# Seven products per weight pair: which accumulator banks share a tile, and how far TensorE's written order reaches

## The chip, the cores and the metric

One core of one Trainium2 chip runs the whole program. The metric is device time in microseconds (us), the median over several runs of the kernel; beside it stands one profiled execution, from which all rows below are read.

## The reference, cut to what matters

The reference is one layer of a streaming encoder over 1024 frames of width 1024: a normalisation, one wide input projection, three token mixers (HGRN2, mLSTM, Mamba-2), three sigmoid branch gates, an output projection, and a gated MLP with a causal convolution. Two products of it matter here:

```
gates = sigmoid(h @ w_in[:, gate columns])                 # 24 blocks of 128 columns
u = causal_dwconv(rmsnorm(x) @ w_up, ffn_conv_w, b)        # 44 blocks of 128 columns
x = x + (silu(u_g) * u_v) @ w_down
```

Both multiply a fixed activation matrix (1024 x 1024) by blocks of 128 weight columns, in float32.

## The kernel before

**Precision.** Each float32 operand is split into a high and a low part (`split`, L98 to L100: a ScalarE cast at L99 for the high part, a VectorE subtraction at L100 for the low one), and each product is three TensorE products: high times high, high times low, low times high.

**Pairs.** Most blocks of the gates (16 of 24) and of the up-projection (38 of 44) are computed two at a time by `pair_gemm`, as a 2 x 2 block product in seven products in place of eight (the Strassen-Winograd scheme). There are 8 pairs in the gate stage (`gate_pairs`) and 19 in the up stage (`up_pairs`). A product (`product`, L166 to L172) is 12 matmuls of 128x512, all recorded at L171, so a pair is 84 of them. In `seven` they are, in order, here called P1 to P7:

- P1 into bank x; `keep` (L188, ScalarE) copies x to the SBUF tile u0
- P2 into bank y; VectorE (L183) adds y and u0 into the first half of the output block `oa`
- P3 on top of x; `keep` copies x to u1
- P4 into bank z; VectorE adds z to u1
- P5 on top of x; `keep` copies x to u2; VectorE adds z and u2 into the second half of `ob`
- P6 into bank v; VectorE adds v and u1 into the second half of `oa`
- P7 on top of x; ScalarE copies x (L192) into the first half of `ob`

P1 and P2 use the weight tiles `wa`, P3 and P4 the tiles `s12`, P5 and P6 the tiles `s34`, P7 the tiles `qb`. `operands` (L142 to L164) makes these: two loads by SyncE's queue, the splits, and four VectorE sums and differences of weights (L160). `wa` and `s12` take turns in two buffers of one pool (`ws`), so the `wa` of one pair lies where that of the pair before lay, and can be cast when that pair's P2 has ended. After a pair, the gate stage applies a sigmoid (L832), the up stage the convolution of both blocks (ScalarE L601, VectorE L605), a SiLU (L958) and a product (L959), and each stores its result.

**Tiles in PSUM.** There are two pools: `pg` with 2 buffers of two banks (name `ps_g`) and `pm` with 4 buffers of one bank (name `ps_m`). A pair takes one `ps_g` tile, whose halves are x and y, and two `ps_m` tiles, z and v.

**The order of the work.** The framework's scheduler sets the order of the instructions on each engine ahead of the run, by a model of their times, and puts in the waits that the tiles' reads and writes ask for. Inside `manual_schedule` the instructions of the engines named are kept in the order in which they are written. Here the block holds one pair's seven products, for TensorE alone, so that the scheduler may still place matmuls from outside the block (another pair's among them) between them. `weight` and `operands` run at a raised priority.

The instruction before and after the pair stages on TensorE is L136 (`steps`), the plain product of one block, into `ps_g` tiles. Line L1001 is the VectorE addition that empties such a tile in `down`.

Of the kernel before, what the change touches and what calls it, by code (L numbers as in the profile page):

```python
# [9 lines left out]
F32 = mybir.dt.float32  # L10
# [8 lines left out]
P = 128  # L19
# [3 lines left out]
HALF = 512  # L23
# [24 lines left out]
class Trunk:  # L48
# [125 lines left out]
    def pair_gemm(self, pool, srcs, outs):  # L174

        nc = self.nc
        wa, s12, s34, qb = self.operands(pool, srcs)
        ps = self.pg.tile([P, T], F32, name="ps_g")
        x, y = ps[:, 0:HALF], ps[:, HALF:]
        z, v = (self.pm.tile([P, HALF], F32, name="ps_m") for _ in range(2))  # L180
        oa, ob = outs
        tmp = lambda: pool.tile([P, HALF], F32, name="u", bufs=4)
        add = lambda out, p, q: nc.vector.tensor_tensor(out=out, in0=p, in1=q, op=ALU.add)  # L183
        u = []

        def keep():
            u.append(tmp())
            nc.scalar.copy(out=u[-1], in_=x)  # L188

        with self.tc.manual_schedule(engines={mybir.EngineType.PE}):  # L190
            self.seven(wa, s12, s34, qb, (x, y, z, v), u, keep, add, oa, ob)
        nc.scalar.copy(out=ob[:, 0:HALF], in_=x)  # L192

    def seven(self, wa, s12, s34, qb, banks, u, keep, add, oa, ob):
        b11, b21, b22, t1, t2, t3, t4 = self.bs
# [645 lines left out]
            self.keep(self.gate_d[i], g)  # L841

    def gate_pairs(self, pool, some):
        for i in some:
            cs = [pool.tile([P, T], F32, name="c", bufs=3) for _ in range(2)]
            self.pair_gemm(pool, [self.ins["w_gate"][i + j] for j in range(2)], cs)
            for j in range(2):
                self.gate_end(i + j, cs[j])
# [120 lines left out]
            self.act(f, us)  # L969

    def up_pairs(self, pool, fs):
        for f in fs:
            ns = (2 * f, 2 * f + 1)
            cs = [pool.tile([P, T], F32, name="c", bufs=3) for _ in ns]
            self.pair_gemm(pool, [self.ins["w_up"][n] for n in ns], cs)
            us = []
            for n, c in zip(ns, cs):
                us.append(self.gp.tile([P, T], F32, name="gate", bufs=3))
                self.up_conv(us[-1], c, n)
            self.act(f, us)  # L980
# [264 lines left out]
```

## Time and profile before

| what | value |
|---|---|
| runs | 2537.37 us median of 3 (2536.49 to 2537.75) |
| the profiled execution | 2535.01 us, its span 2533.2 us |
| granted TensorE clock, mean over the span | 0.995 |
| TensorE busy | 2474.8 us of the span (98%) |
| VectorE, ScalarE busy | 1503.5 us (59%), 1003.5 us (40%) |

The gate pairs run from about 1255 to 1422 us of the span, the up pairs from about 1883 to 2277 us. A matmul row lasts longer (389 ns) than the distance to the next one, as the ends are modelled and matmuls overlap; so time on TensorE is read from start to start.

### The profile page before, as it was taken

How to read it: one execution, taken by the hardware profiler on the slowest of the kernel's cores; microseconds unless marked ns; L12 is line 12 of the kernel's file. 1: busy time of each engine (PE TensorE's matmuls, PEld its weight loads, DVE VectorE, ACT ScalarE, POOL GpSimd, SP SyncE). 2: the span in 40 equal slices, each digit the busy share in tenths (PEclk: the TensorE clock that was granted, in tenths of full speed). 3: DMA queues.
4: the chain of work that ended last, by engine and by line, in shares of the span. 5: the costliest groups of instructions: out<-in, count | busy, mean ns of one | idle time of the engine just before them, and what ended most of it. 6: DMA issues, size and time to landing. Idle time of an engine off the chain costs nothing.

```text
span 2533.2 us, 31151 instructions
## 1 busy us (share of the span) xinstructions
PE 2474.8 (98%) x12980; PEld 2111.6 (83%) x12980; DVE 1503.5 (59%) x1888; ACT 1003.5 (40%) x1233; POOL 62.2 (2%) x99
## 2 busy tenths in 40 slices
PE   8999999999999999999999999999999999999998
PEld 6898989898898898899877888888777777778886
DVE  6676767774344366766844324444687777775445
ACT  5444445553334255446433312212344444441112
POOL 2000000000000000000000000000000000000000
PEclk8999999999999999999999999999999999999999
DMA  5111111111111122122323444444222222244321
GB/s 215 34 41 44 42 42 34 53 59 58 67 67 60 49 92 80 61 69 92 150 100 105 162 134 156 156 135 150 100 76 82 75 75 77 82 136 147 108 75 67
DMA packets 64141, 228.63 MB, mean 90 GB/s; under 512 B 7400, under 2 KB 8040, under 8 KB 63232
## 3 DMA queue, kind: packets, MB, share of 16 engines
q1 hardware_dynamic: 52352, 181.54, 21.6%
q0 software_dynamic: 11648, 45.09, 4.5%
q8 instruction: 102, 1.67, 0.3%
q14 instruction: 39, 0.32, 0.0%
HBM read 177.23 MB, written 49.38 MB: 89 GB/s over the span
## 4 chain that ended last, share of the span: by engine, by line
PE 94%; DVE 2%; ACT 2%; issue 1%; DMA 1%; POOL 0%; DVEq 0%; ACTq 0%
PE ps_g L136 48%; PE ps_g L171 14%; PE ps_g L270 10%; PE ps_m L171 6%; PE ps_m L136 5%; PE ps_m L464 3%; PE ps_m L797 1%; ACT w_hi L99 1%; PE ps_m L270 1%; PE ps_m L473 1%; PE ps_m L708 1%; PE ps_m L679 1%; PE ps_m L483 1%; PE ps_m L436 0%; PE ps_m L659 0%
## 5 line engine op out<-in xcount | busy, mean ns | idle before, releaser
L136 PE MATMUL ps_g<-h,w_hi 128*128 128x512 f32 x2080 | 585.0, 397 | 5.9 <-DVE h L100 3.9
L99 ACT CAST w_hi<-w_raw 128x1024 fp32r<-128x1024 f32 x209 | 218.6, 1046 | 720.4 <-PE ps_g L136 540.6
L136 PEld LDWEIGHTS ps_g<-h,w_hi 128*128 128x128 f32 x2080 | 387.7, 188 | 86.0 <-DVE h L100 4.7
L100 DVE TENSOR_TENSOR w_lo<-w_raw,w_hi 128x1024 fp32r<-128x1024 f32 x209 | 255.1, 1221 | 169.7 <-ACT w_hi L99 168.4
L136 PE MATMUL ps_g<-h,w_lo 128*128 128x512 f32 x1040 | 331.9, 395 | 0.0
L270 PE MATMUL ps_g<-w_hi,h 128*128 128x256 f32 x1408 | 261.0, 284 | 0.0
L136 PE MATMUL ps_g<-p_hi,w_hi 128*128 128x512 f32 x768 | 239.9, 390 | 5.0 <-ACT w_hi L99 2.1
L136 PE MATMUL ps_g<-p_lo,w_hi 128*128 128x512 f32 x768 | 239.2, 389 | 0.8 <-DVE p_lo L100 0.8
L136 PE MATMUL ps_g<-p_hi,w_lo 128*128 128x512 f32 x768 | 239.3, 389 | 0.0
L136 PEld LDWEIGHTS ps_g<-h,w_lo 128*128 128x128 f32 x1040 | 195.4, 188 | 40.2
L270 PEld LDWEIGHTS ps_g<-w_hi,h 128*128 128x128 f32 x1408 | 221.2, 192 | 0.6
L270 PE MATMUL ps_g<-w_lo,h 128*128 128x256 f32 x704 | 200.1, 284 | 0.0
L136 PEld LDWEIGHTS ps_g<-p_hi,w_hi 128*128 128x128 f32 x768 | 143.8, 188 | 36.9 <-ACT w_hi L99 3.4
L136 PEld LDWEIGHTS ps_g<-p_lo,w_hi 128*128 128x128 f32 x768 | 144.1, 188 | 31.3 <-DVE p_lo L100 1.1
L136 PEld LDWEIGHTS ps_g<-p_hi,w_lo 128*128 128x128 f32 x768 | 144.1, 188 | 30.1 <-DVE w_lo L100 0.3
L270 PEld LDWEIGHTS ps_g<-w_lo,h 128*128 128x128 f32 x704 | 134.9, 192 | 0.5
L188 ACT COPY u<-ps_g 128x512 f32<-128x512 f32 x81 | 45.8, 589 | 188.6 <-PE ps_g L171 186.0
L183 DVE TENSOR_TENSOR c<-ps_m,u 128x512 f32<-128x512 f32 x54 | 37.4, 692 | 129.5 <-ACT u L188 92.9
L1001 DVE TENSOR_TENSOR x<-ps_g,x 128x1024 f32<-128x1024 f32 x40 | 49.0, 1225 | 89.3 <-PE ps_g L136 88.9
L605 DVE SCALAR_TENSOR_TENSOR gate<-c,c_vec,gate 128x1023 f32<-128x1023 f32 x76 | 95.8, 1279 | 2.0 <-ACT gate L601 1.9
L100 DVE TENSOR_TENSOR p_lo<-w_raw,p_hi 128x1024 fp32r<-128x1024 f32 x48 | 58.3, 1224 | 43.5 <-ACT p_hi L99 42.8
L99 ACT CAST p_hi<-w_raw 128x1024 fp32r<-128x1024 f32 x48 | 50.4, 1050 | 84.3 <-DMA w_raw<-act_dram 30.4
(311 smaller groups left out, 4068.8 us busy)
## 6 DMA issues: line engine op xcount, KB each, us to landing
w_raw<-w_up SPq DMA_DIRECT2D x44, 512.0 KB, 3.3
w_raw<-w_hg SPq DMA_DIRECT2D x24, 512.0 KB, 3.3
w_raw<-w_v SPq DMA_DIRECT2D x24, 512.0 KB, 3.4
ta<-rows SPq DMA_DIRECT2D x24, 512.0 KB, 4.4
w_raw<-w_gate SPq DMA_DIRECT2D x24, 512.0 KB, 3.5
w_raw<-w_br SPq DMA_DIRECT2D x24, 512.0 KB, 3.8
w_raw<-y_dram SPq DMA_DIRECT2D x24, 512.0 KB, 4.4
gate<-gate_dram SPq DMA_DIRECT2D x24, 512.0 KB, 4.4
```

What stands on the lines that cost most here:

```text
L99: self.nc.scalar.copy(out=hi, in_=src)
L100: (eng or self.nc.vector).tensor_tensor(out=lo, in0=src, in1=hi.bitcast(F32), op=ALU.subtract)
L136: self.nc.tensor.matmul(out=out, lhsT=w[:, ks], rhs=rhs(part, kt, ts), start=kt == 0 and w is hi and part == 0, stop=kt == kts - 1 and w i ...
L171: self.nc.tensor.matmul(out=out, lhsT=w[x][:, ks], rhs=b[y][k], start=start and k == i == 0, stop=stop and k == 3 and i == 2, skip_group_c ...
L183: add = lambda out, p, q: nc.vector.tensor_tensor(out=out, in0=p, in1=q, op=ALU.add)
L188: nc.scalar.copy(out=u[-1], in_=x)
L270: self.nc.tensor.matmul(out=out, lhsT=self.h[hf][part][:, 4 * i + k, o:o + P], rhs=w[:, ks], start=start and k == 0 and w is hi and part = ...
L464: nc.tensor.matmul(out=pa[0:m, c], lhsT=z[:, c * P:c * P + m], rhs=part(1)[:, c], start=True, stop=True)
L473: nc.tensor.matmul(out=pa[:, j], lhsT=c3(k)[:, c + j], rhs=qs[:, c + j], start=True, stop=True)
L483: nc.tensor.matmul(out=po[:, j], lhsT=A[:, c], rhs=v[:, c, vs], start=True, stop=c == 0)
L605: end = nc.vector.scalar_tensor_tensor(out=out[:, a:ts.stop], in0=ps[:, a - d:ts.stop - d], scalar=w(d), in1=out[:, a:ts.stop], op0=ALU.mu ...
L1001: nc.vector.tensor_tensor(out=x2[j], in0=ps, in1=x2[j], op=ALU.add)
```

## The change

In `pair_gemm` the halves of the `ps_g` tile become y and v, and the two `ps_m` tiles become x and z. The number of tiles and banks that a pair takes from each pool stays. The `manual_schedule` block moves from around one call of `seven` to a generator, `in_order`, which wraps the loop over all pairs of a stage: TensorE's instructions of all 8 (or 19) pairs are kept in the order in which they are written, P1 to P7 of one pair, then P1 to P7 of the next. The block now also encloses the loads, splits, convolutions and stores of the loop's body, on other engines than the one that it names.

```diff
         ps = self.pg.tile([P, T], F32, name="ps_g")
-        x, y = ps[:, 0:HALF], ps[:, HALF:]
-        z, v = (self.pm.tile([P, HALF], F32, name="ps_m") for _ in range(2))
+        y, v = ps[:, 0:HALF], ps[:, HALF:]
+        x, z = (self.pm.tile([P, HALF], F32, name="ps_m") for _ in range(2))
...
+        self.seven(wa, s12, s34, qb, (x, y, z, v), u, keep, add, oa, ob)
+        nc.scalar.copy(out=ob[:, 0:HALF], in_=x)
+
+    def in_order(self, jobs):
+
         with self.tc.manual_schedule(engines={mybir.EngineType.PE}):
-            self.seven(wa, s12, s34, qb, (x, y, z, v), u, keep, add, oa, ob)
-        nc.scalar.copy(out=ob[:, 0:HALF], in_=x)
+            yield from jobs
...
     def gate_pairs(self, pool, some):
-        for i in some:
+        for i in self.in_order(some):
...
     def up_pairs(self, pool, fs):
-        for f in fs:
+        for f in self.in_order(fs):
```

## Rows read from the trace of the kernel before

**Rows 1.** The page: its head, and TensorE's line of part 1.
```profile
span 2533.2 us, 31151 instructions
...
PE 2474.8 (98%) x12980; PEld 2111.6 (83%) x12980; DVE 1503.5 (59%) x1888; ACT 1003.5 (40%) x1233; POOL 62.2 (2%) x99
```
**Rows 2.** Waits of TensorE in the gate pairs: total us, times, longest.
```profile
PE ps_g L171 <- DVE c L183: 5.5, 7, 0.8
PE ps_g L171 <- ACT w_hi L99: 0.9, 1, 0.9
PE ps_g L171 <- ACT u L188: 0.7, 1, 0.7
```
**Rows 3.** The same view of the up pairs.
```profile
PE ps_g L171 <- ACT w_hi L99: 16.5, 17, 1.9
PE ps_g L136 <- ACT w_hi L99: 2.1, 1, 2.1
```
**Rows 4.** Timeline, TensorE, up pairs: start, duration, operation, [idle before, releaser].
```profile
1910.78 0.50 PE L171 MATMUL ps_g<-p_hi,w_hi 128*128 128x512 f32 x1 [0.91 <-ACT w_hi L99]
...
1965.54 2.88 PE L171 MATMUL ps_g<-t,w_b 128*128 128x512 f32 x12
1968.26 0.39 PE L171 MATMUL ps_g<-p_hi,w_hi 128*128 128x512 f32 x1
...
1970.75 0.39 PE L171 MATMUL ps_g<-p_hi,w_lo 128*128 128x512 f32 x1
1972.05 0.50 PE L171 MATMUL ps_g<-p_hi,w_hi 128*128 128x512 f32 x1 [0.91 <-ACT w_hi L99]
...
1972.68 0.73 PE L171 MATMUL ps_g<-t,w_hi 128*128 128x512 f32 x2
...
2217.10 0.50 PE L171 MATMUL ps_g<-p_hi,w_hi 128*128 128x512 f32 x1 [0.91 <-ACT w_hi L99]
```
**Rows 5.** Timeline, ScalarE, the same up pair.
```profile
1968.23 0.62 ACT L99 CAST w_b<-w_raw 128x512 fp32r<-128x512 f32 x1 [0.52 <-PE ps_g L171]
1968.76 0.58 ACT L192 COPY c<-ps_g 128x512 f32<-128x512 f32 x1
1969.37 1.25 ACT L601 ACTIVATE gate<-c,c_vec 128x1024 f32<-128x1024 f32 x1
1970.95 1.04 ACT L99 CAST w_hi<-w_raw 128x1024 fp32r<-128x1024 f32 x1 [0.33 <-PE ps_g L171]
1971.90 1.05 ACT L958 ACTIVATE gate<-gate 128x1024 f32<-128x1024 f32 x1
1975.73 0.59 ACT L188 COPY u<-ps_g 128x512 f32<-128x512 f32 x1 [2.77 <-PE ps_g L171]
```
**Rows 6.** Timeline, VectorE, the same up pair.
```profile
1969.55 2.47 DVE L605 SCALAR_TENSOR_TENSOR gate<-c,c_vec,gate 128x1022 f32<-128x1022 f32 x2
1971.94 0.69 DVE L183 TENSOR_TENSOR c<-ps_g,u 128x512 f32<-128x512 f32 x1
```
**Rows 7.** Timeline, TensorE, the first up pair.
```profile
1886.65 0.50 PE L171 MATMUL ps_g<-p_hi,w_hi 128*128 128x512 f32 x1 [0.68 <-ACT u L188]
...
1890.54 0.74 PE L171 MATMUL ps_g<-t,w_hi 128*128 128x512 f32 x2 [0.85 <-DVE c L183]
```
**Rows 8.** Timeline, TensorE, gate pairs: the second and the seventh pair's P3.
```profile
1282.62 0.72 PE L171 MATMUL ps_g<-t,w_hi 128*128 128x512 f32 x2 [0.78 <-DVE c L183]
...
1383.29 0.50 PE L171 MATMUL ps_g<-t,w_hi 128*128 128x512 f32 x1 [0.78 <-DVE c L183]
```
**Rows 9.** Windows of one pair: length; PE, PEld, DVE, ACT, POOL busy; clock; DMA.
```profile
1302.76:1322.89 20.13, 19.35 (x84) 15.68 (x84) 9.90 (x12) 7.93 (x11) 1.07 (x2) 1.00 0.30 105
1951.64:1972.05 20.41, 19.50 (x84) 15.62 (x85) 15.24 (x18) 9.29 (x12) 0.53 (x1) 1.00 0.21 78
```
**Rows 10.** Timeline, TensorE, where the last up pair meets the down-projection (L136).
```profile
2259.95 0.74 PE L136 MATMUL ps_g<-p_hi,w_hi 128*128 128x512 f32 x2 [2.06 <-ACT w_hi L99]
...
2281.91 0.73 PE L136 MATMUL ps_g<-p_hi,w_hi 128*128 128x512 f32 x2 [1.61 <-DVE x L1001]
```
**Rows 11.** Timeline, ScalarE, then VectorE, first gate pair: the high and low part of its `s12`.
```profile
1258.72 1.05 ACT L99 CAST w_hi<-w_raw 128x1024 fp32r<-128x1024 f32 x1 [0.19 <-DVE w_raw L160]
...
1259.80 1.23 DVE L100 TENSOR_TENSOR w_lo<-w_raw,w_hi 128x1024 fp32r<-128x1024 f32 x1 [0.39 <-ACT w_hi L99]
```

## The prediction

> **What bounds the kernel now.** I read the head of the page first: TensorE is busy 2474.8 of 2533.2 us [rows 1], so the end is set by TensorE's own work and by the holes in it, and a change that adds and removes no matmul can only move holes. Then the waits of TensorE, taken for the two stretches that the change touches [rows 2, 3]: there the reader sees three releasers only, the cast of a weight (`w_hi` L99), the addition at L183 and the copy at L188; no DMA. Then the timeline, to see where in a pair the holes lie [rows 4 to 8].
>
> A product starts 2.72 us after the one before (P7 at 1965.54, P2 at 1968.26) [rows 4], so a pair without holes takes 7 x 2.72 = 19.04 us. The up pairs come every 20.42 us, (2217.10 - 1910.78) / 15, and the gate pairs every 20.13 us, (1383.29 - 1282.62) / 5 [rows 4, 8]. So an up pair has 1.38 us of holes and a gate pair 1.09. A hole costs some 0.3 us more than the row's idle time (1.09 against 0.78), since rows overlap; I add 0.3 to each hole below.
>
> What the up pair's hole is: after P2 has ended (last start 1970.75) two matmuls of the next pair's P1 come, then P3 (1972.68) [rows 4]. Those two stand there because the program's order puts them there. Their weight can only be cast when P2 has let go of the buffer: the cast begins at 1970.95 and takes 1.04 [rows 5], and TensorE sits 0.91 us. P3 could not have gone either: in the gate pairs, where it stands directly behind P2, it waits 0.78 us for L183, the addition that reads y [rows 8]. That addition ran at 1971.94, behind two L605 [rows 6]. But P3 writes x, not y. And in the first up pair P2, which writes y, waits 0.68 us for the copy of x [rows 7]. In both cases the waiting product shares nothing with its releaser but the tile whose halves are x and y. I read that as waits kept by tile.
>
> **The change, part by part.**
>
> *x leaves y's tile.* P2 no longer shares a tile with the copy of x, nor P3 with the addition out of y. P3 still must wait for the copy u0, as must P5 for u1 and P7 for u2. Each has a whole other product in front of it: 2.72 us, against a copy of 0.59 [rows 5] that can start about when that product starts. The cover is some 2.1 us, one 1.25 us activation can run into it free, two cannot. The new partners y and v: P6 writes v while the tile's other half was read by the addition after P2, which is 3 products or 8.2 us earlier; nothing. z keeps a tile of its own. Buffers: x now takes `ps_m`, two of four per pair, so it falls to the tile of two pairs back, whose last reader (L192) is a whole pair old; nothing.
>
> *Order over all pairs.* P1 of a pair now stands behind P7 of the one before, and not in the hole after P2. No instruction is added. Its cast becomes possible when the last P2 ends, 5 products or 13.6 us ahead of its use, against a cast of 1.04 and a subtraction of about 1.2 [rows 5, 11]. The casts of `s12` and `s34` have the same distance from the P4 and P6 that free their buffers. No load is moved past another: SyncE's queue holds loads one pair ahead before and after.
>
> What goes, with 0.3 per single hole:
> - up pairs: 17 waits for the cast. 16 regular ones at 1.38 = 22.1; the 17th is the long one, 1.9 in place of 0.91 [rows 3], 2.4.
> - first up pair: 0.68 + 0.85 + 0.6 = 2.1 [rows 7].
> - after the last up pair's P2 the down-projection's matmuls take the hole and wait 2.06 for their own cast [rows 10]: 2.4.
> - gate pairs: 7 waits for L183 at 1.09 = 7.6; the first pair's two others, 0.9 + 0.7 + 0.6 = 2.2 [rows 2].
> - together 38.8.
>
> What stays or comes:
> - first gate pair: P3 would come up about 1260.5, and its `s12` is cast by 1259.8 and subtracted by 1261.0 [rows 11], while the third matmul wants it at 1260.9. 0 to 0.6; I take 0.3.
> - behind the last P7, all eight columns of the first down group now follow at once, and VectorE has the last pair's convolutions to do beside emptying them. Now that costs 1.61 + 0.3 [rows 10], with one column done ahead. It could shrink to 0 (-1.9) or cost one L605 and one L1001 more (+2.5). I take +1.5, nearer to the upper end as more columns meet the same VectorE.
> - VectorE and ScalarE have 15.24 and 9.29 us of work in an up pair [rows 9]; over 19.04 us that is 80% and 49%. Neither becomes the bound, and no matmul hangs closely on VectorE any more.
>
> Sum: 38.8 - 0.3 - 1.5 = 37.0. The profiled execution took 2535.0 us (span 2533.2), which becomes 2498; the median of the runs lies 2.4 above it, so 2537.4 - 37 = 2500.5 us.
>
> On the tile reading a rule of the Trainium skill speaks against the first part: the page "PSUM — Partial Sum Buffer" (Terms, PSUM bank) lets TensorE's write and ScalarE's read clash only in one and the same bank. x and y lay in different banks before as well, so by that rule nothing is won by giving them other tiles, and the 0.68 us that P2 waited for the copy of x must have another cause. That would be the case of the rival "the waits stay", below. The trace shows the wait, not its cause; I hold it to be the program's, not the chip's.
>
> **The rivals.**
>
> *The copies come late.* With P1 directly behind P7, the ScalarE queue between them and u0 holds the cast `w_b` 0.62, the copy L192 0.58, L601 1.25 and the SiLU 1.05 [rows 5]: 3.5 us from P7's end, and then u0 ends at 4.1, where P3 is due at 5.44. That fits. But the SiLU needs VectorE's convolutions. If it stands ahead of u0 and waits for two L605 (2.47) [rows 6], u0 ends at 0.62 + 0.58 + 1.25 + 2.47 + 1.05 + 0.59 = 6.6, with four handovers of 0.2 at 7.4: P3 is 1.9 us late in each of 19 up pairs, 36 us, and the time is 2537; with one L605 in the way less, 0.7 late, 2514. For it: the SiLU stands before the u copy in that queue today. Against: there it started without any idle time, and the queue is laid out from times that now let the copy be ready first. Slower only if u0 ends later than 7.4 us after P7.
>
> *The order does not hold across pairs* and P1 keeps its place behind P2. Then the up pairs keep their hole, the gate pairs lose theirs (9.8): 2528. For: a matmul from outside a block is placed into it today. Against: the new block holds all pairs.
>
> *The waits stay* (the slower one). If P2's wait for the copy and P3's for the addition come from something other than the tile, the strict order lays them bare in every pair, as the first up pair has them today: 2.1 us [rows 7] x 27 = 57 us, against 38.8 removed, with the 1.8 that comes: 2537.4 + 57 - 37 = 2557. It decides from 37 / 27 = 1.4 us per pair. Against: P2's operands are older than P1's, and the releaser reads only x.
>
> **How the numbers follow.** My forecast 0.81, with a range of its own from 2495 (both open ends nil or below, 2 of slack) to 2508 (0.3 us of late copies in every pair, or the tail at its upper end with it). Late copies 0.09, 2508 to 2537; order not held 0.03, 2528; waits stay 0.07, 2557. The range 2494 to 2519 leaves out the last two, most of the late copies and a few hundredths of the forecast: under 2 in 10. 0.2% (5 us) is about what a measurement of this kernel can tell from no change: faster is 0.81 + 0.03 + 0.05 of the late copies = 0.89, same 0.04, slower 0.07.
>
> **What would show it.** In the waits of TensorE over the up pairs, the rows for `w_hi` L99 and L183 are gone, and pairs follow at 19.1 us in both stages. The product P1 into `ps_m` follows P7 directly. ScalarE's u copies begin within 0.3 us of a product's end. If the SiLU row shows idle time released by VectorE and L171 waits for L188, the first rival holds; if P2 shows a hole of 0.7 released by L188, the third. The forecast is wrong if the pair's period stays above 19.6 us, or if holes of more than 5 us appear elsewhere on TensorE.

## The result and the profile after

The changed kernel takes 2498.73 us (median of 4 runs, 2498.43 to 2500.11) against 2537.36 before: a ratio of 0.9849, 95% interval 0.9832 to 0.9866. Its profiled execution took 2498.8 us, its span 2497.0. In the experiments below the same program was run again, with 2499.3 us. The medians differ by 38.6 us, the two profiled spans by 36.2: the profiled execution before was 2.4 us faster than its median, the one after 0.1 us slower.

The head of the page after; it answers to [rows 1].

```profile
span 2497.0 us, 31129 instructions
...
PE 2464.3 (99%) x12980; PEld 2116.6 (85%) x12980; DVE 1508.2 (60%) x1888; ACT 1005.8 (40%) x1233; POOL 62.2 (2%) x99
```

As many matmuls as before (12980) end 36.2 us earlier. From the starts of the first and last L171 of each stage: the gate pairs went from 166.50 to 158.46 us, the up pairs from 393.12 to 364.25, what lies between the stages stayed at 461.6, and what follows went from 257.0 to 256.6. The gate pairs begin 1.1 us later, at 1256.13; in the second run of the same program they begin at 1255.50, so two runs of one program differ by 0.6 us here.

The waits of TensorE after, first over the gate pairs, then over the up pairs and the start of the down-projection. These two rows are all that is left of [rows 2, 3].

```profile
PE ps_m L171 <- DVE w_lo L100: 1.5, 1, 1.5
```
```profile
PE ps_g L136 <- DVE x L1005: 2.2, 1, 2.2
```

TensorE's timeline after, from P7 of one up pair to P1 of the next but one; it answers to [rows 4].

```profile
1949.59 2.88 PE L171 MATMUL ps_m<-t,w_b 128*128 128x512 f32 x12
1952.31 0.39 PE L171 MATMUL ps_m<-p_hi,w_hi 128*128 128x512 f32 x1
...
1955.03 0.39 PE L171 MATMUL ps_g<-p_hi,w_hi 128*128 128x512 f32 x1
...
1957.75 0.61 PE L171 MATMUL ps_m<-t,w_hi 128*128 128x512 f32 x2
...
1971.35 0.39 PE L171 MATMUL ps_m<-p_hi,w_hi 128*128 128x512 f32 x1
```

P7, P1, P2 and P3 start 2.72 us apart without an idle note, and P1 comes again after 1971.35 - 1952.31 = 19.04 us: 7 x 2.72, a pair without a hole. The window of that pair, with the columns of [rows 9]:

```profile
1952.31:1971.35 19.04, 19.04 (x85) 15.77 (x84) 15.55 (x18) 9.39 (x12) 0.53 (x1) 1.00 0.24 83
```

ScalarE and VectorE in the same pair, against [rows 5, 6]:

```profile
1952.29 0.62 ACT L99 CAST w_b<-w_raw 128x512 fp32r<-128x512 f32 x1 [0.52 <-PE ps_m L171]
1952.81 0.58 ACT L191 COPY c<-ps_m 128x512 f32<-128x512 f32 x1
1953.43 1.25 ACT L605 ACTIVATE gate<-c,c_vec 128x1024 f32<-128x1024 f32 x1
1955.23 0.59 ACT L188 COPY u<-ps_m 128x512 f32<-128x512 f32 x1 [0.56 <-PE ps_m L171]
1955.72 1.06 ACT L962 ACTIVATE gate<-gate 128x1024 f32<-128x1024 f32 x1
```
```profile
1953.60 3.79 DVE L609 SCALAR_TENSOR_TENSOR gate<-c,c_vec,gate 128x1022 f32<-128x1022 f32 x3
1957.50 1.23 DVE L963 TENSOR_TENSOR gate<-gate 128x1024 f32<-128x1024 f32 x1
1958.64 0.68 DVE L183 TENSOR_TENSOR c<-ps_g,u 128x512 f32<-128x512 f32 x1
```

The addition out of y (L183) now runs at 1958.64, 0.9 us after P3 has begun. In the old tiles P3 would have waited for it; here it needs the copy alone, which ended at 1955.82. And the SiLU (L962) now stands behind the copy.

### The profile page after: what moved, and what is told of

It is laid out like the page before. It is cut to its first block, busy times and chain, and to the rows that moved or that the text cites. A ratio compares the mean times of both kernels' runs of the same rounds, so it can differ in the third digit from the quotient of the medians.

```text
span 2497.0 us, 31129 instructions
## 1 busy us (share of the span) xinstructions
PE 2464.3 (99%) x12980; PEld 2116.6 (85%) x12980; DVE 1508.2 (60%) x1888; ACT 1005.8 (40%) x1233; POOL 62.2 (2%) x99
## 4 chain that ended last, share of the span: by engine, by line
PE 96%; DVE 2%; issue 1%; ACT 1%; DMA 0%; SPq 0%; DVEq 0%; ACTq 0%
PE ps_g L136 48%; PE ps_m L171 15%; PE ps_g L274 10%; PE ps_g L171 6%; PE ps_m L136 5%; PE ps_m L468 3%; PE ps_m L801 1%; PE ps_m L274 1%; PE ps_m L477 1%; PE ps_m L712 1%; PE ps_m L683 1%; PE ps_m L487 1%; PE ps_m L440 1%; PE ps_m L663 0%; PE ps_m L685 0%
## 5 line engine op out<-in xcount | busy, mean ns | idle before, releaser
L136 PE MATMUL ps_g<-h,w_hi 128*128 128x512 f32 x2080 | 585.4, 398 | 5.8 <-DVE h L100 3.9
L136 PEld LDWEIGHTS ps_g<-h,w_hi 128*128 128x128 f32 x2080 | 388.2, 189 | 85.6 <-DVE h L100 4.7
L136 PE MATMUL ps_g<-h,w_lo 128*128 128x512 f32 x1040 | 332.3, 395 | 0.0
L136 PE MATMUL ps_g<-p_hi,w_hi 128*128 128x512 f32 x768 | 239.5, 390 | 2.8 <-DVE x L1005 2.2
L136 PE MATMUL ps_g<-p_lo,w_hi 128*128 128x512 f32 x768 | 239.2, 389 | 0.8 <-DVE p_lo L100 0.8
L136 PE MATMUL ps_g<-p_hi,w_lo 128*128 128x512 f32 x768 | 239.4, 389 | 0.0
L136 PEld LDWEIGHTS ps_g<-h,w_lo 128*128 128x128 f32 x1040 | 195.6, 188 | 40.3
L136 PEld LDWEIGHTS ps_g<-p_hi,w_hi 128*128 128x128 f32 x768 | 144.0, 188 | 34.0 <-DVE x L1005 2.6
L136 PEld LDWEIGHTS ps_g<-p_lo,w_hi 128*128 128x128 f32 x768 | 144.2, 188 | 31.2 <-DVE p_lo L100 1.1
L136 PEld LDWEIGHTS ps_g<-p_hi,w_lo 128*128 128x128 f32 x768 | 144.1, 188 | 30.2 <-DVE w_lo L100 0.3
L171 PE MATMUL ps_m<-t,w_hi 128*128 128x512 f32 x432 | 133.0, 389 | 0.0
L171 PEld LDWEIGHTS ps_m<-t,w_hi 128*128 128x128 f32 x432 | 81.1, 188 | 16.8
L188 ACT COPY u<-ps_m 128x512 f32<-128x512 f32 x81 | 47.6, 588 | 117.4 <-PE ps_m L171 117.4
L171 PE MATMUL ps_m<-t,w_lo 128*128 128x512 f32 x216 | 84.1, 390 | 1.5 <-DVE w_lo L100 1.5
```

The lines of the kernel that those rows point to most:

```text
L136: self.nc.tensor.matmul(out=out, lhsT=w[:, ks], rhs=rhs(part, kt, ts), start=kt == 0 and w is hi and part == 0, stop=kt == kts - 1 and w i ...
L171: self.nc.tensor.matmul(out=out, lhsT=w[x][:, ks], rhs=b[y][k], start=start and k == i == 0, stop=stop and k == 3 and i == 2, skip_group_c ...
```

## The experiments

All were run against the kernel before, which took 2537.6 to 2538.0 us beside them.

**The tiles without the order.** From the changed kernel, the block goes back around one pair:

```diff
+        with self.tc.manual_schedule(engines={mybir.EngineType.PE}):
+            self.seven(wa, s12, s34, qb, (x, y, z, v), u, keep, add, oa, ob)
...
-        for i in self.in_order(some):
+        for i in some:
```

> The new tiles, with the written order around one pair's products only, as before. Theory T (the holes came from waits that go by tile; x sharing a tile with y made P3 wait for the addition at L183, and only that hole let the next P1 in behind P2): with x in its own tile P3 can follow P2 at once, so no hole opens, the pairs run at 19.1 us in both stages, and the time is that of the changed kernel, 2499 within 5 us. Rival O (the order over all pairs is what does it): P1 of the next pair keeps its place behind P2 in the up pairs and waits there for its cast, 1.38 x 19 = 26 us stay and the gate pairs' holes go: about 2525 us.

2499.46 us (ratio 0.985, 0.9834 to 0.9867): the whole gain. The two holes that are left are those of the changed kernel (waits of TensorE, the two longest):

```profile
PE ps_g L136 <- DVE x L1006: 2.1, 1, 2.1
PE ps_m L171 <- DVE w_lo L100: 1.5, 1, 1.5
```

TensorE's order is not that of the changed kernel, though. In every pair that has a next one, the next pair's P1 and P2 stand, cut in pieces, before P5 and before P7, and in the gate pairs and about half of the up pairs behind P7 too. With x out of y's tile that costs nothing. Rival O is out.

**The order without the tiles.**

```diff
-        y, v = ps[:, 0:HALF], ps[:, HALF:]
-        x, z = (self.pm.tile([P, HALF], F32, name="ps_m") for _ in range(2))
+        x, y = ps[:, 0:HALF], ps[:, HALF:]
+        z, v = (self.pm.tile([P, HALF], F32, name="ps_m") for _ in range(2))
```

> The old tiles (x and y in one, z and v in tiles of their own), with the order written over all pairs. Theory T: every pair shows the two holes of the first up pair of the kernel before, P2 behind the copy of x (0.68 + 0.3) and P3 behind the addition out of y (0.85 + 0.3, more where VectorE is still at the convolutions): 2.1 us or more in each of 27 pairs, 57 us above the changed kernel, 2556 us or later, slower than before. Rival B (waits go by bank, the tiles don't matter): no such holes, 2499 us.

2555.44 us, slower than before (ratio 1.0074, 1.0059 to 1.0089). TensorE's waits, and its timeline in one up pair:

```profile
PE ps_g L171 <- ACT u L188: 20.7, 27, 2.2
PE ps_g L171 <- DVE c L183: 20.1, 25, 0.9
```
```profile
2000.35 0.50 PE L171 MATMUL ps_g<-p_hi,w_hi 128*128 128x512 f32 x1 [0.68 <-ACT u L188]
...
2004.16 0.74 PE L171 MATMUL ps_g<-t,w_hi 128*128 128x512 f32 x2 [0.78 <-DVE c L183]
```

The two holes of the first up pair of before [rows 7] come back in nearly every pair: P2 waits for the copy in all 27, P3 for the addition in 25 (not in the first gate pair and the last up pair). A pair takes 21.13 us, 2.09 more than 19.04; 27 of them make 56.4, and the kernel is 56.7 us slower than the changed one.

**x with v in one tile**, order over all pairs:

```diff
-        y, v = ps[:, 0:HALF], ps[:, HALF:]
-        x, z = (self.pm.tile([P, HALF], F32, name="ps_m") for _ in range(2))
+        x, v = ps[:, 0:HALF], ps[:, HALF:]
+        y, z = (self.pm.tile([P, HALF], F32, name="ps_m") for _ in range(2))
```

> Order over all pairs; x shares its tile with v, and y and z have tiles of their own. Every bank is still a separate one. Theory T: P6, which writes v, waits for the copy u2 of x that follows P5 (0.7 + 0.3), and P7, which writes x, waits for the addition out of v that follows P6 (0.8 + 0.3): 2.1 us in each of 27 pairs, 2556 us. P2 and P3 wait for nothing. Rival B (by bank): 2499 us, no hole.

2552.36 us (ratio 1.006, 1.0045 to 1.0075). Timeline of TensorE in an up pair:

```profile
2009.92 0.50 PE L171 MATMUL ps_g<-p_hi,w_s 128*128 128x512 f32 x1 [0.68 <-ACT u L188]
...
2013.73 0.50 PE L171 MATMUL ps_g<-t,w_b 128*128 128x512 f32 x1 [0.79 <-DVE c L183]
```

The waiters are now P6 (`p_hi,w_s`) and P7 (`t,w_b`); P2 and P3 wait for nothing, but for the first gate pair's P3 (1.5 us, for a weight). The holes have moved to the products that now share a tile with a bank just read, with the same length, while each bank is separate in all three kernels. So the waits go by tile, not by bank.

**y with z in one tile**, x and v alone (the same two lines, with `y, z` from `ps` and `x, v` from `self.pm`):

> Order over all pairs; x and v have tiles of their own, y and z share one. So the bank of the fifth product has no tile of its own, unlike in the changed kernel. Theory T: P4, which writes z, must wait for the addition out of y that follows P2; one whole product (2.72 us) stands between, against some 1.8 us until that addition has ended in an up pair; nothing is left over, 2499 us within 3. Rival Z (z needs a tile of its own): P4 waits in each up pair, 0.5 us or more, 2509 us or later.

2499.0 us (ratio 0.985, 0.9836 to 0.9865), and no wait of L171 in the up pairs. The fifth product's bank needs no tile of its own. What counts is that two products that follow each other don't share one: P2 and P4 share one here, and the product between them covers the wait.

**Copies made three times and six times.** In the changed kernel:

```diff
-            nc.scalar.copy(out=u[-1], in_=x)
+            for _ in range(3):
+                nc.scalar.copy(out=u[-1], in_=x)
```

> The changed kernel, with each copy of x (u0, u1, u2) made three times into the same tile, which adds two copies of some 0.49 us to each of 81. By the forecast's cover: the copies of a product end some 0.35 + 3 x 0.49 = 1.8 us after the next product's start, the third product is due at 2.72, nothing is late: 2499 us within 4. By the rival that the copies already come late, each added copy is paid in full: 81 x 0.98 = 79 us, 2578 us; in part: anything above 2505.

2509.96 us: a miss, by 7 us beyond its bound. The gate pairs stayed 19.04 us apart. The up pairs came some 19.36 apart, but the last began 23.3 us after the one before it: there a cast for the down-projection and the SiLU both stood before the last copy, and P3 waited 2.4 us. ScalarE in one up pair:

```profile
1994.11 0.59 ACT L189 COPY u<-ps_m 128x512 f32<-128x512 f32 x1 [0.56 <-PE ps_m L171]
1994.59 1.06 ACT L963 ACTIVATE gate<-gate 128x1024 f32<-128x1024 f32 x1
1995.55 1.20 ACT L189 COPY u<-ps_m 128x512 f32<-128x512 f32 x2
```

The queue put the SiLU between the copies of u0. They end at 1996.75, and P3, due 2.72 after P2's start at 1993.91, came at 1996.81 in place of 1996.63. That is the mechanism of the first rival, at the edge of its cover: two added copies (1.20, where the expectation had 0.98) and a SiLU (1.06) just exceed what is there. Where no SiLU stands between the copies, as in the gate pairs, two added copies are free.

> The changed kernel with each copy of x made six times. By the forecast's cover: 0.35 + 6 x 0.49 = 3.3 us against 2.72, so 0.57 late, and 0.1 for the restart, in each of 81 places: 54 us, about 2553 us, with waits of L171 for L188 of some 0.4 to 0.5 us each, that weren't there before. If the cover were twice as long (5.4 us), 2499 still; if it were 1 us, 2700 or more.

2772.84 us, 220 us beyond the expectation. ScalarE, then TensorE, in one up pair; then the window of that product, and of the whole stage; then the waits of TensorE over both stages:

```profile
2107.69 2.45 ACT L189 COPY u<-ps_m 128x512 f32<-128x512 f32 x4 [3.10 <-PE ps_m L171]
2110.19 1.04 ACT L99 CAST w_hi<-w_raw 128x1024 fp32r<-128x1024 f32 x1
2111.14 1.20 ACT L189 COPY u<-ps_m 128x512 f32<-128x512 f32 x2
```
```profile
2112.38 4.61 PE L171 MATMUL ps_m<-t,w_s 128*128 128x512 f32 x12 [2.01 <-ACT u L189]
```
```profile
2112.38:2116.83 4.45, 4.45 (x12) 3.53 (x13) 0.71 (x2) 0.00 (x0) 0.00 (x0) 0.62 0.39 118
```
```profile
1949.00:2514.00 565.00, 435.93 (x1620) 335.65 (x1618) 302.77 (x323) 341.32 (x497) 10.10 (x19) 0.90 0.17 60
```
```profile
PE ps_m L171 <- ACT u L189: 175.9, 77, 3.6
```

Three things were left out of the expectation. A copy behind a copy costs 0.61 us (four take 2.45) and not 0.49, so six alone would be over 1 us late and not 0.57. A cast stands between them in the queue, so TensorE sits 2.0 us before P5; over both stages it waits 175.9 us in 77 places. And the granted clock falls: 0.62 in this product, which takes 4.45 us to the next one's start in place of 2.72, 0.90 over the up stage and 0.92 over the 242 us of the gate stage. An estimate from these: 175.9 + 77 x 0.3 for the holes and 0.10 x 565 + 0.08 x 242 for the clock make 275 us, against 273.5 measured over the changed kernel.

**The hole behind the last pair.** First, one x tile in another pool:

```diff
-                        x2.append(pool.tile([P, T], F32, name="x2", bufs=KT))
+                        x2.append(self.gp.tile([P, T], F32, name="gate", bufs=3) if j == 0 else
+                                  pool.tile([P, T], F32, name="x2", bufs=KT))
```

> The changed kernel, with the first of the eight x tiles of the down-projection in a buffer of the gate pool, which doesn't have to wait for the last pair's operands to be let go. Theory F (the hole of 2.2 us behind the last pair is the first addition L1005 waiting for that tile's load, issued at 2240.8 only when P7 has ended): the load is issued before P7, the hole shrinks to 0.5 us or less, and the time is 2 us lower, 2496.7 us. Rival V (VectorE's convolutions L609 hold the addition): the hole stays within 0.5 us of 2.2 and the time does too.

2499.81 us, and a hole of 2.28. It decides nothing between the two: SyncE's queue, here, still sends the load (into `gate`) at 2240.80, behind two of the others and when P7 had ended.

```profile
2239.83 0.80 SPq L245 DMA_DIRECT2D x<-x_dram  x2
2240.80 0.32 SPq L245 DMA_DIRECT2D gate<-x_dram  x1
```

> The changed kernel itself beside the others, for a comparison on one chip: 2498.7 us within 2.

2499.3 us. Then, in the changed kernel, two of the eight loads go into weight buffers, ahead of the others:

```diff
+            early = [self.wr.tile([P, T], F32, name="w_raw") for _ in range(2 if first == 0 else 0)]
+            for j, t in enumerate(early):
+                self.fetch(t, self.x2_d[j])
...
-                        self.fetch(x2[j], self.x2_d[j])
-                    nc.vector.tensor_tensor(out=x2[j], in0=ps, in1=x2[j], op=ALU.add)
+                        was = early[j] if j < 2 else x2[j]
+                        if j >= 2:
+                            self.fetch(was, self.x2_d[j])
+                    else:
+                        was = x2[j]
+                    nc.vector.tensor_tensor(out=x2[j], in0=ps, in1=was, op=ALU.add)
```

> The changed kernel; the first two of the eight x tiles that the down-projection adds to are loaded into two of the four weight buffers, behind the first activations' loads, so that they need not wait until the last pair's operands are let go. In the run before, the load meant to be early still went out behind P7, so it told nothing. Theory F (the hole of 2.2 us behind the last pair is L1005 waiting for that load): the two loads land before P7 ends, the hole is 0.6 us or less, 2 us are gained, 2497 us. Rival V (VectorE's convolutions hold the addition): the hole stays within 0.5 us of 2.2, 2499 us.

The first addition runs at 2241.03, with P7 started at 2237.91 in both kernels (it ran at 2244.43 in the changed one), and two small holes take the place of the one (VectorE, then TensorE):

```profile
2241.03 1.22 DVE L1012 TENSOR_TENSOR x<-ps_g,w_raw 128x1024 f32<-128x1024 f32 x1
```
```profile
2241.17 0.73 PE L136 MATMUL ps_g<-p_hi,w_hi 128*128 128x512 f32 x2 [0.38 <-DVE c L183]
...
2247.24 0.73 PE L136 MATMUL ps_g<-p_hi,w_hi 128*128 128x512 f32 x2 [0.31 <-DVE x L1012]
```

So the hole was the load (theory F). The 2 us that were expected of it did not come. Counted from the last L171, the matmuls behind the holes come 1.0 to 1.1 us earlier than in the changed kernel, and the end of the program 0.2 to 0.3 us earlier (256.27 us behind it, against 256.60 and 256.52 in the changed kernel's two profiles). The time is 2498.32 us (2496.9 to 2498.54), against 2499.3 for the changed kernel in another batch on another chip; 1 us is less than such a measurement can tell.

**The tiles without any written order.** In the changed kernel, both loops go without `in_order`, so that no `manual_schedule` is left around a pair or a stage:

> The new tiles with no written order at all, neither for a pair nor for a stage. Theory T (once x is alone in its tile nothing on TensorE waits, whatever the order among the pairs): the pairs still run at 19.1 us and the time is 2499 within 5 us. Rival O (the order inside a pair is needed): the scheduler brings products that use x next to each other, each such place costs a copy, 0.95 us, once or more in 27 pairs: 2525 us or later.

2501.64 us (ratio 0.9859, 0.9842 to 0.9875). The scheduler mixes the products of neighbouring pairs throughout (P7 in the middle of the next pair's P3 and P4, P6 before P5), and yet no product waits in either stage, not even in the first gate pair. The one hole is behind the last pair, longer by 2.7 us (the loads of the x tiles leave at 2242.46 there, 1.6 us later than in the changed kernel):

```profile
PE ps_g L136 <- DVE x L1005: 4.9, 1, 4.9
```

## Why the prediction was right, and where its steps were not

The time (2500.5 forecast, though its sum gives 2500.4; 2498.7 measured), the periods (19.1 forecast, 19.04 measured in both stages) and the reading behind them held: the waits in [rows 7, 8] were kept by tile. They moved with the tiles in three arrangements of the same separate banks, so it is the tile that decides them. The rule that the prediction set against this reading, of the Trainium skill's page "PSUM — Partial Sum Buffer" (Terms, PSUM bank), is about two engines in one bank at once on the chip; no run here tested it.

Point by point:

- *x leaves y's tile.* Held, and it is the whole gain (2499.5 us alone). It was forecast as one of two parts.
- *Order over all pairs.* This step failed in what it credits. The prediction let the cast waits of the up pairs (22.1 + 2.4 us) go because P1 was moved behind P7. In the kernel with the tiles alone they go as well, though P1 and P2 stay among the products of the pair before: the two matmuls of P1 that had stood behind P2 now stand further on, where no cast is waited for. A likely reason, argued and not shown, is that P3, held up by L183, left a gap in the scheduler's model that those two filled. The order alone costs 18 us, by 2555.4 against 2537.6.
- *The waits stay.* The price of this rival, 2.1 us per pair and 2557, is what the old tiles under the new order cost: 2.09 and 2555.4. That a strict order lays the waits bare in every pair was right. Its condition, a cause other than the tile, did not hold, so the new tiles prevent it.
- *The copies come late.* Not in the changed kernel. The cover of 2.1 us held for two more copies without the SiLU, and was used up by them where the SiLU came in between.
- *First gate pair*, 0.3 forecast, 1.5 idle and some 0.3 around it measured. `s12`'s high part was ready at 1260.88, but its subtraction stood in VectorE's queue behind an addition that waits for P2's end. TensorE, ScalarE and VectorE there:

```profile
1263.72 0.50 PE L171 MATMUL ps_m<-t,w_lo 128*128 128x512 f32 x1 [1.53 <-DVE w_lo L100]
```
```profile
1259.83 1.05 ACT L99 CAST w_hi<-w_raw 128x1024 fp32r<-128x1024 f32 x1 [0.19 <-DVE w_raw L160]
```
```profile
1261.84 0.69 DVE L183 TENSOR_TENSOR c<-ps_g,u 128x512 f32<-128x512 f32 x1 [1.32 <-PE ps_g L171]
1262.45 2.35 DVE L100 TENSOR_TENSOR w_lo<-w_raw,w_hi 128x1024 fp32r<-128x1024 f32 x2
```

In the kernel before, the same two stood the other way round [rows 11]. The size was read from a queue order that the change itself rewrote. With this, the gate pairs gave 8.0 us in place of 9.5; the up pairs gave 28.9 against 29.0.

- *Behind the last P7*, +1.5 forecast, +0.6 measured (2.2 against 1.61 in [rows 10]), and for another reason than the one given. That the sum came within 2 us owes something to this and the term before being off in opposite directions. One column (12 matmuls of L136) still runs ahead of P7, so they do not all follow at once. And the addition does not wait for VectorE's convolutions but for its x tile, whose load leaves at 2240.8 (SyncE, VectorE, TensorE):

```profile
2240.83 3.89 SPq L245 DMA_DIRECT2D x<-x_dram  x8
```
```profile
2244.43 1.22 DVE L1005 TENSOR_TENSOR x<-ps_g,x 128x1024 f32<-128x1024 f32 x1 [3.52 <-DMA x<-x_dram]
```
```profile
2245.71 0.73 PE L136 MATMUL ps_g<-p_hi,w_hi 128*128 128x512 f32 x2 [2.20 <-DVE x L1005]
```

So the sum came out right with one of its two reasons wrong: had the order been made alone, on the strength of that step, the kernel would have become slower, as the run with the order alone did.

What stays open is the first gate pair's hole. To turn the two VectorE instructions round was not tried; in the kernel without any written order they stand as here, and TensorE fills the time with other matmuls.

## What to carry to other kernels

Where two products that follow each other write into halves of one tile, each waits, in this framework, for whoever still reads the other half, though the banks differ. Give such neighbours separate tiles, and let two products share a tile only if a whole product lies between them. Before you write an order by hand, look for a wait that may have made the scheduler choose an odd one: here the order written down by itself made the kernel slower, and with the wait removed it was not needed. When an edit has two parts, a forecast for each alone costs one line and shows which of them carries the sum.

## What the runs showed of the hardware

The granted clock can fall behind a single hole of some 2 us, and need not. Behind the last pair TensorE waits 2.1 to 2.3 us in several of these kernels. First the hole and the next few us in the kernel with the tiles alone, then the same stretch of the changed kernel, whose hole is the one of 2.20 us shown above:

```profile
2244.53 0.73 PE L136 MATMUL ps_g<-p_hi,w_hi 128*128 128x512 f32 x2 [2.12 <-DVE x L1006]
```
```profile
2244.00:2250.00 6.00, 5.47 (x17) 4.36 (x18) 4.98 (x5) 0.00 (x0) 0.53 (x1) 0.72 1.04 400
```
```profile
2244.00:2250.00 6.00, 4.29 (x19) 3.56 (x20) 5.57 (x5) 0.00 (x0) 0.00 (x0) 1.00 1.02 414
```

The clock fell behind 2.12 us and stayed at 1.00 behind 2.20. It fell behind 2.28 us with the first load moved (0.72 too), and not behind 2.10 in the changed kernel's second run. In those two kernels the program ended some 2 us later, counted from the last L171 (258.7 and 259.1 against 256.6 and 256.5).

With six copies TensorE waited three times per pair, mostly 2.0 to 3.6 us, and the clock went between its two levels (1.2 and 2.4 GHz): 0.62 on average in the product that followed a 2.01 us hole, and 0.90 over the up stage, against 1.00 over the up pairs of the changed kernel and of before. The holes of 0.7 to 0.8 us, two per pair, in the kernel with the order alone did not do that: the clock is 1.00 over both its stages.
